# Square products in the fox gates of a two-layer hybrid trunk

## The chip, the cores and the metric

One core of a Trainium2 chip runs the whole program. The metric is device time in microseconds (us) of one execution. PE is the matmul engine (TensorE), DVE is VectorE, ACT is ScalarE, POOL is GpSimd, SP is the engine whose queue issues the weight loads.

## The reference, cut to what matters

The model has two layers, 256 rows, a width of 2048, all float32. The change touches how one half of the mixer's gate, `sigmoid(g_fox)`, is computed:

```
a = rms_norm(x, n_mix_pre)
proj = a @ w_in                      # the last 4096 columns of it are g_fox, g_nsa (2048 each)
o_fox, o_nsa = fox_attention(...), nsa_attention(...)      # 256 x 1024 each
mix = sigmoid(g_fox) * (o_fox @ w_up_fox) + sigmoid(g_nsa) * (o_nsa @ w_up_nsa)
x = x + rms_norm(mix @ w_out, n_mix_post)
a = rms_norm(x, n_ffn_pre)
h = (silu(a @ w_gate) * (a @ w_up)) @ w_down
return x + rms_norm(h, n_ffn_post)
```

## The kernel before, in words

**Split products.** Every float32 operand is split into a high and a low part (a fast matmul type each), and each product becomes three matmuls, high times high, high times low, low times high (lines 394 to 396 in `part`, 441 to 443 in `product`). The rows of an activation are in two tiles of 128, `t` = 0 and 1. `aT[t][c]` holds the mixer's input transposed: four tiles of 128 k rows, high and low. The 2048 inner rows are 16 k tiles.

**Weight units.** `stream` (line 242) cuts a weight into units of two k tiles by 512 columns (512 KB). SP loads a unit into one of five raw buffers; ACT copies it to the high part `wh`, DVE subtracts it for the low part `wl` (lines 162 and 172, which are those of the helpers `copy` and `split`). How far ahead of PE this is written into the program is set by `budget`: `room["ahead"]` units ahead at most, `room["slots"]` live buffers at most. `ensure(i)` is called once for each unit and row tile that PE uses, and emits a step or two of the next units' splits.

**A chunk** (`chunk`, line 408) is one block of 512 columns: both row tiles in two PSUM banks, 96 matmuls for 16 k tiles. After each part (6 matmuls) `pump` takes one step of a side generator.

**A square** (`square_chunk`, line 445) works on two column blocks at once. Two k tiles, two row tiles and two column blocks are a 2 by 2 by 2 product; instead of 8 products it takes 7 (of 3 matmuls each) with sums of rows and sums of weights as operands. A "pair" is the two units of both column blocks with the same two k tiles. The first `SEVEN` = 2 pairs are squares, unless `lead` puts some plain pairs ahead of them. Then `between` gathers the 7 banks into the four results (`gather`, line 665), and the other pairs follow plainly, 24 matmuls each, into four banks. The sums of weights are made by `split_sums` (line 259) in two steps: step 1 makes the parts of the left unit (`wl`) and of one tile of the right one (`wq`) and four sums in the raw buffers (lines 268 and 276 to 279 in the profile); step 2 makes the parts of the two sums, `xh`, `xl`, `yh`, `yl`, all under the names `wh` and `wl`. The products come in the order 6, 5, 7, ..., and product 6 takes `yh` and `yl`. The sums of rows are made by `left_gen` (line 1177).

**Alike rows.** A square mixes two row tiles, whose rows have different norm factors. In the feed-forward stage `powers`, `spread` and `alike` (lines 1398 to 1422) therefore multiply `aT2` by the power of two in each row's factor, in place, before squares are used.

**The mixer's gates and ups.** The loop at line 1207 goes through `n` (nsa) and `f` (fox). For each of four column blocks `c` of 512 it runs the gate chunk (16 k tiles, 96 matmuls; ACT takes the sigmoid out of PSUM, line 1216) and the up chunk (8 k tiles of `oT`, 48 matmuls; DVE multiplies it by the gate, line 1221 for n, 1223 and 1224 for f, where the product is added into `mix`). After each f block `mix_gen` transposes `mix` for the output projection (PSUM tile `mT`, SBUF tile `mixT`); for c = 3 it rests two pumps first (`REST`). The output projection `out` begins with two plain pairs (`lead` = 2). Its row sums come from `left_gen(1, mixT, ...)`: the tiles `full` and `sm`.

**The end of a layer.** `tail` closes the last down projection with `turn(0)` and `turn(1)`, generators which make the next layer's `aT`, one per row tile; PE waits for those tiles at the start of layer two.

Engines run their own instructions in the order in which the program was written; the order is set by hand (`tc.manual_schedule`), by `pump`, `ensure` and `need`.

Of the kernel before, what the change touches and what calls it, by code (L numbers as in the profile page):

```python
# [38 lines left out]
KT = DM // 128  # L39
# [9 lines left out]
ROOM_OUT = 10  # L49
ROOM_LATE = 22  # L50
REST = 2
ROOM_MIX = 16
ROOM_DOWN = 10

# [54 lines left out]
def trunk(ctx: ExitStack, tc: tile.TileContext, I: dict, consts: bass.AP, out: bass.AP):  # L109
# [879 lines left out]
        yield  # L989


    def squares(left, right, k0, nk, own=False, skew=0, lead=0):


        ks = range(k0, k0 + nk, 2)
        pairs = [[None, None] for k in ks]
        level = len(ks) - skew
        order = [(p, i) for p in range(level) for i in range(2)]
        order += [(p, i) for i in range(2) for p in range(level, len(ks))]
        for p, i in order:  # L1000
            w, col = (left, right)[i]
            pairs[p][i] = stream(w, ks[p], 2, col, 512)[0]
        for g, u in pairs[lead:lead + SEVEN]:
            units[g].update(block=u, own=own)
            units[u]["second"] = True
        return pairs

    def plan(l):
# [38 lines left out]
    def run_layer(l, P, aT, rs, turns, x_src, x_mid, x_next):  # L1047
# [126 lines left out]

        sums = {}

        def left_gen(c, rows, home):

            n = 2 * SEVEN
# [21 lines left out]
                pass  # L1201

        def lhs_s(f, p):
            i = (5, 6, 7, 3).index(f)
            return sums["hi"][:, i, p, :], sums["lo"][:, i, p, :]

        for nm in ("n", "f"):
            if nm == "f":
                budget(8)
            for c in range(4):  # L1210
                ga, ua = P[nm][c]
                sgc = [None, None]

                def gate_evac(t, p):
                    sgc[t] = staged([128, 512], F32, "sgc")
                    act.activation(sgc[t], p, AF.Sigmoid, scale=rs[t][:, 0:1])

                def up_evac(t, p):
                    m = mix[t][c // 2][:, (c % 2) * 512:(c % 2) * 512 + 512]
                    if nm == "n":  # L1220
                        dve.tensor_tensor(m, p, sgc[t], op=OP.mult)
                    else:
                        dve.tensor_tensor(sgc[t], p, sgc[t], op=OP.mult)
                        dve.tensor_tensor(m, m, sgc[t], op=OP.add)

                chunk(ga, lhs_a, gate_evac)
                if nm == "f" and c == 3:
                    room["slots"], room["ahead"] = ROOM_MIX, 5
                if c == 0:
                    drain()  # L1230
                    if nm == "n":
                        for h in range(FH):
                            waiting.append(fox_head(L, h))
                chunk(ua, lhs_o(L["onsa"] if nm == "n" else L["ofox"]), up_evac)
                if nm == "f":
                    made = [Once(mix_gen(t, c, REST * (c == 3))) for t in range(2)]
                    waiting.extend(made)
                    if c == 2:
                        lefts = Once(left_gen(1, mixT, slot))
                        waiting.append(lefts)  # L1240

        close_stage()
        open_stage(f"ffn{l}")

        def one(shape, dt, name):
            return staged(shape, dt, name, 1)

        def tagged(tag, bufs=2):

            return lambda shape, dt, name: staged(shape, dt, tag, bufs)  # L1250


        due = deque()
# [31 lines left out]
        def tail(couples, lhs, yg, partial, wait, gen, loads, xs, gb, last=False, lead=0):  # L1285
# [64 lines left out]
        lefts.need("end")  # L1350

        def load_late():
            load_rows(x_src, tagged("wq"))()
# [35 lines left out]
            waiting.extend(late)  # L1389
            late.clear()  # L1390

        rest = [None, None]

        p2 = [None, None]

        def powers(t):
            p2[t], rest[t] = staged([128, 1], F32, "p2"), staged([128, 1], F32, "rest")
            r = rs2[t][:, 0:1].bitcast(I32)  # L1400
            dve.tensor_scalar(p2[t].bitcast(I32), r, 0x7F800000, None, op0=OP.bitwise_and)
            dve.tensor_scalar(rest[t].bitcast(I32), r, 0x007FFFFF, 0x3F800000, op0=OP.bitwise_and, op1=OP.bitwise_or)

        def spread():
            for _ in range(6):
                yield
            tp = side_ps("rb")
            for t in range(2):
                pe.transpose(tp[:, t * 128:(t + 1) * 128], p2[t].to_broadcast([128, 128]), ident)
            sums["rb"] = staged([128, 2, 128], F32, "rb", 1)  # L1410
            dve.tensor_copy(sums["rb"], tp[:, 0:256].rearrange("p (t n) -> p t n", t=2))
            yield "rb"

        def alike(have, j):

            if j < 4 or j % 2:
                return
            have.need("rb")
            rb = sums["rb"]
            for c, t in [(c, t) for c in range(j // 2 - 1 if j > 4 else 0, j // 2) for t in range(2)]:  # L1420
                a = aT2[t][c].rearrange("p k s n -> p (k s) n")
                dve.tensor_tensor(a, f32(a), rb[:, t:t + 1, :].to_broadcast([128, 8, 128]), op=OP.mult)

        (a0, a1), (b0, b1) = FFN_PARTS

        def ffn(c):
# [4 lines left out]
            if c < 2:  # L1431
                ga, ua = P["ffn"][c]
                scale = rest if c else rs2

                def gate_evac(t, p):
                    if c == 0:
                        turns2[t].need("rs")
                        powers(t)
                    act.activation(hb[:, t], p, AF.Silu, scale=scale[t][:, 0:1])

                def up_evac(t, p):
                    dve.scalar_tensor_tensor(hb[:, t], p, scale[t][:, 0:1], hb[:, t], op0=OP.mult, op1=OP.mult)

                if c:
                    chunk(ga, lhs_a2, gate_evac)
                    left_sums(0, aT2, one)
                    chunk(ua, lhs_a2, up_evac)
                else:
                    chunk(ga, lhs_a2, gate_evac, before=wait_a2, head=8)
                    drain()  # L1450
                    budget(8, 8)
                    have = Once(spread())
                    waiting.append(have)
                    chunk(ua, lhs_a2, up_evac, after=lambda j: alike(have, j))
                    alike(have, 8)
# [151 lines left out]
```

## Time and profile before

| | us |
|---|---|
| median of 3 runs | 2807.79 (2807.76 to 2807.98) |
| profiled execution, device time | 2807.83 |
| its span in the trace | 2806.0 |
| PE busy | 2792.1 |
| DVE busy | 1995.7 |
| ACT busy | 1426.3 |
| POOL busy | 106.3 |

The profiled execution is 0.04 us above the median; 1.8 us of it lie outside the traced span. Busy times are averages over stages that differ. PE's matmuls overlap in the trace: each is shown with 390 ns, but in a steady stream they start closer together, so a group's busy time divided by its count is less than the length of one row.

### The profile page before, as it was taken

To read this page: it belongs to the slowest core of one execution; us is meant where nothing else is said; L and a number is where in the kernel's file an instruction comes from. 1 tells how busy PE (TensorE), PEld (TensorE's weight loads), DVE (VectorE), ACT (ScalarE), POOL (GpSimd) and SP (SyncE) were. 2 spreads that over 40 slices of the span, in tenths; PEclk is the share of its full clock that TensorE was granted. 3 is DMA by queue.
4 is the path that set the end of the run, shared out by engine and by line. 5 is a ranking of instruction groups with operands and counts; after the bars stand their busy time and mean duration, and the time that the engine had idled before them with its cause. 6 is when DMAs were issued, how large, how long until landed. Compare 5 with 4: busy or idle time off the path is not lost.

```text
span 2806.0 us, 35561 instructions
## 1 busy us (share of the span) xinstructions
PE 2792.1 (100%) x13114; PEld 2338.9 (83%) x13114; DVE 1995.7 (71%) x2578; ACT 1426.3 (51%) x2022; POOL 106.3 (4%) x191
## 2 busy tenths in 40 slices
PE   9999999999999999999999999999999999999998
PEld 8988888888888888888899888888888888888887
DVE  6666665576888788788666566555768887887885
ACT  6555554455554455445455455544564544544453
POOL 0100000001000000000011000000020000000000
PEclk9999999999999999999999999999999999999999
DMA  7673446566565566556666644455765655665564
GB/s 249 201 261 116 140 151 199 196 222 224 195 224 170 167 220 217 175 191 220 215 201 224 218 130 147 154 198 188 239 219 190 214 178 183 217 202 173 188 218 165
DMA packets 291806, 547.04 MB, mean 195 GB/s; under 512 B 17264, under 2 KB 59568, under 8 KB 291632
## 3 DMA queue, kind: packets, MB, share of 16 engines
q1 hardware_dynamic: 289856, 543.56, 58.9%
q8 instruction: 103, 1.69, 0.2%
q10 hardware_dynamic: 1776, 1.21, 0.1%
q14 instruction: 71, 0.58, 0.1%
HBM read 536.31 MB, written 8.39 MB: 194 GB/s over the span
## 4 chain that ended last, share of the span: by engine, by line
PE 98%; DVE 1%; DMA 0%; ACT 0%; issue 0%; POOL 0%; SPq 0%; DVEq 0%; ACTq 0%; POOLq 0%
PE acc L443 16%; PE acc L441 16%; PE acc L442 16%; PE acc L394 15%; PE acc L396 15%; PE acc L395 15%; PE hT L526 1%; PE ph L881 1%; PE ph L880 1%; PE tp L526 0%; PE ns L706 0%; PE ns L705 0%; PE no L699 0%; PE no L698 0%; PE no L700 0%; DMA raw<-in_w_in 0%
## 5 line engine op out<-in xcount | busy, mean ns | idle before, releaser
L162 ACT ACTIVATE wh<-raw 128x1024 fp32r<-128x1024 f32 (+1 forms) x1064 | 1067.6, 1044 | 470.1 <-DVE raw L277 158.1
L172 DVE TENSOR_TENSOR wl<-raw,wh 128x1024 fp32r<-128x1024 f32 (+1 forms) x896 | 1049.3, 1208 | 295.4 <-ACT wh L162 266.6
L394 PE MATMUL acc<-wh,aT 128*128 128x512 f32 (+1 forms) x1534 | 598.0, 390 | 0.0
L396 PE MATMUL acc<-wh,aT 128*128 128x512 f32 (+1 forms) x1534 | 585.1, 381 | 1.0 <-DVE aT L575 1.0
L395 PE MATMUL acc<-wl,aT 128*128 128x512 f32 (+1 forms) x1534 | 584.9, 381 | 0.1
L441 PE MATMUL acc<-wh,aT 128*128 128x512 f32 x972 | 381.5, 392 | 0.0
L443 PE MATMUL acc<-wh,aT 128*128 128x512 f32 x972 | 379.0, 390 | 0.0
L442 PE MATMUL acc<-wl,aT 128*128 128x512 f32 x972 | 378.4, 389 | 0.0
L396 PEld LDWEIGHTS acc<-wh,aT 128*128 128x128 f32 x1534 | 287.9, 188 | 51.5 <-DVE aT L575 1.7
L394 PEld LDWEIGHTS acc<-wh,aT 128*128 128x128 f32 x1534 | 288.4, 188 | 43.9 <-issue 0.8
L395 PEld LDWEIGHTS acc<-wl,aT 128*128 128x128 f32 x1534 | 288.6, 188 | 41.8 <-DVE wl L172 0.3
L441 PE MATMUL acc<-wh,hT 128*128 128x512 f32 x624 | 243.9, 391 | 0.0
L443 PE MATMUL acc<-wh,hT 128*128 128x512 f32 x624 | 243.3, 390 | 0.0
L442 PE MATMUL acc<-wl,hT 128*128 128x512 f32 x624 | 243.0, 389 | 0.0
L268 DVE TENSOR_TENSOR wl<-raw,wh 128x1024 fp32r<-128x1024 f32 x168 | 202.4, 1221 | 22.6 <-PE acc L442 9.9
L443 PEld LDWEIGHTS acc<-wh,aT 128*128 128x128 f32 x972 | 182.4, 188 | 38.6
L442 PEld LDWEIGHTS acc<-wl,aT 128*128 128x128 f32 x972 | 182.6, 188 | 37.4
L441 PEld LDWEIGHTS acc<-wh,aT 128*128 128x128 f32 x972 | 182.5, 188 | 37.0
L442 PEld LDWEIGHTS acc<-wl,hT 128*128 128x128 f32 x624 | 117.2, 188 | 24.7
L443 PEld LDWEIGHTS acc<-wh,hT 128*128 128x128 f32 x624 | 117.1, 188 | 24.6
L441 PEld LDWEIGHTS acc<-wh,hT 128*128 128x128 f32 x624 | 117.2, 188 | 24.4
L394 PE MATMUL acc<-wh,oT 128*128 128x512 f32 x256 | 102.0, 399 | 0.0
(351 smaller groups left out, 3082.7 us busy)
## 6 DMA issues: line engine op xcount, KB each, us to landing
raw<-in_w_in SPq DMA_DIRECT2D x224, 512.0 KB, 4.6
raw<-in_w_ffn_gate SPq DMA_DIRECT2D x176, 512.0 KB, 4.8
raw<-in_w_ffn_up SPq DMA_DIRECT2D x176, 512.0 KB, 4.7
raw<-in_w_ffn_down SPq DMA_DIRECT2D x176, 512.0 KB, 5.7
raw<-in_w_in SPq DMA_DIRECT2D x96, 432.0 KB, 4.4
raw<-in_w_out SPq DMA_DIRECT2D x64, 512.0 KB, 5.7
raw<-in_w_up_nsa SPq DMA_DIRECT2D x32, 512.0 KB, 4.6
raw<-in_w_up_fox SPq DMA_DIRECT2D x32, 512.0 KB, 4.9
```

The source lines that it names most:

```text
L162: act.activation(o, i, AF.Copy, scale=1.0 if scale is None else scale)
L172: dve.tensor_tensor(lo, src, f32(hi), op=OP.subtract)
L268: dve.tensor_tensor(lo, src, f32(hi), op=OP.subtract)
L394: pe.matmul(ps[t][:, :n], ah, hi, start=first, stop=False)
L395: pe.matmul(ps[t][:, :n], ah, lo, start=False, stop=False)
L396: pe.matmul(ps[t][:, :n], al, hi, start=False, stop=end)
L441: pe.matmul(ps, ah, bh, start=first, stop=False)
L442: pe.matmul(ps, ah, bl, start=False, stop=False)
L443: pe.matmul(ps, al, bh, start=False, stop=last)
L526: pe.transpose(dst[:, j * 128:(j + 1) * 128], s, ident)
L880: pe.matmul(ph[:120, 0:256], b, units[u]["hi"][:, jj, :], start=p == 0, stop=False)
L881: pe.matmul(ph[:120, 0:256], b, units[u]["lo"][:, jj, :], start=False, stop=p == CL - 1)
```

## The change

For the fox gates the four gate chunks become two couples of column blocks, (0, 1) and (2, 3). Each couple is one `square_chunk` with two squares and no lead, then come its two up chunks. The weight sums are marked `own` (their `wq` lives in the common slots). For this `powers`, `spread` and `alike` become methods that take the tiles; they are used on `aT` beside the nsa gates of c = 2, and `left_gen(0, aT, ...)` makes the row sums beside the nsa gates of c = 3. `alike` is 8 multiplications of 128 x 1024 (4, 2, 2 at three places) in each layer; `spread` adds two transposes on PE and one copy on DVE. The split of weights runs up to 6 units ahead in place of 4 in the fox stage. `turn(1)` at a layer's end now first finishes `turn(0)` up to its fourth tile. The wait for the sums of `mixT` moves into `lhs_s`.

```diff
@@ plan
             for c in range(4):
-                a = stream(w, 0, KT, col + 512 * c, 512)
+                a = None
+                if nm == "n":
+                    a = stream(w, 0, KT, col + 512 * c, 512)
+                elif c % 2 == 0:
+                    a = squares((w, col + 512 * c), (w, col + 512 * c + 512), 0, KT, True)
                 P[nm].append((a, stream(I[up][l], 0, 8, 512 * c, 512)))
@@ run_layer
-                chunk(ga, lhs_a, gate_evac)
...
+        scaled = [powers(rs[t]) for t in range(2)]
+        rows_by = [rs[t][:, 0:1] for t in range(2)]
+        for c in range(4):
+            ga, ua = P["n"][c]
...
+            if c == 2:
+                chunk(ga, lhs_a, gate_evac, after=lambda j: alike(aT, have, rb, j))
+                alike(aT, have, rb, 8)
+                rows_by = [v[:, 0:1] for _, v in scaled]
+            else:
+                chunk(ga, lhs_a, gate_evac, beside=left_gen(0, aT, tagged("kT")) if c == 3 else None)
...
+            chunk(ua, lhs_o(L["onsa"]), up_evac)
+        budget(ROOM_F // 2, 6)
+        for c in range(4):
+            ga, ua = P["f"][c]
+            if not c % 2:
...
+                def between(ps):
+                    gather(ps, sg_, tagged("w2", 1)([128, 1, 512], F32, "hu"), False)
+
+                def gate_evac(t, right, p):
+                    o = sg_[t][right]
+                    dve.tensor_tensor(o, p, o, op=OP.add)
+                    act.activation(o, o, AF.Sigmoid, scale=rows_by[t])
+
+                square_chunk(ga, lhs_a, lhs_s, between, gate_evac, together=False)
...
+            if c == 3:
+                room["slots"], room["ahead"] = ROOM_MIX, 5
+            chunk(ua, lhs_o(L["ofox"]), up_evac)
+            made = [Once(mix_gen(t, c, REST * (c == 3))) for t in range(2)]
...
@@ tail, turn
+                if t:
+                    turns[0].need("3")
                 turns[t] = Once(gen(t, ys, ssy[t], xs))
```

Three places show how the rows move. The first is DVE at the start of the fox stage; `mix_2988` and `mix_2990` are the last nsa up block's results for row tiles 0 and 1. Before:

```order
L172 TENSOR_TENSOR wl<-raw,wh 128x1024 x12
L1221 TENSOR_TENSOR mix_2988<-acc_4270,sgc 128x512
L1221 TENSOR_TENSOR mix_2990<-acc_4271,sgc 128x512
L172 TENSOR_TENSOR wl<-raw,wh 128x1024 x13
L1223 TENSOR_TENSOR sgc<-acc_4502,sgc 128x512
```

and after, where lines 269 and 277 to 280 are `split_sums`:

```order
L173 TENSOR_TENSOR wl<-raw,wh 128x1024 x4
L269 TENSOR_TENSOR wl<-raw,wh 128x1024
L269 TENSOR_TENSOR wq<-raw,wq 128x512
L277 TENSOR_TENSOR raw<-raw 128x512
...
L1263 TENSOR_TENSOR mix_2988<-acc_4303,sgc 128x512
L1263 TENSOR_TENSOR mix_2990<-acc_4304,sgc 128x512
L269 TENSOR_TENSOR wl<-raw,wh 128x1024 x3
L269 TENSOR_TENSOR wq<-raw,wq 128x512
L277 TENSOR_TENSOR raw<-raw 128x512
L278 TENSOR_TENSOR raw<-raw 128x512
L279 TENSOR_TENSOR raw<-raw 128x512
L280 TENSOR_TENSOR raw<-raw 128x512
L269 TENSOR_TENSOR wl<-raw,wh 128x1024 x2
```

Step 1 of the first square stands ahead of the two `mix` rows; its step 2 (the first two of the three `wl`), the whole step 1 of the second square and its step 2 (the last two `wl`) stand behind them. The second place is PE at the same point of the program, after the change; `kT` is the tag in which the sums of `aT` lie:

```order
L397 MATMUL acc_4304<-wh,oT 128x512
L442 MATMUL acc_4385<-wh,kT 128x512
L443 MATMUL acc_4385<-wl,kT 128x512
L444 MATMUL acc_4385<-wh,kT 128x512
```

The last up matmul of row tile 1 (`acc_4304`) is followed at once by product 6 of the first square; before, the plain gate chunk stood there. The third place is DVE beside the last fox up chunk, ahead of the output projection; `mix_2988` and `mix_2990` are now the last fox block's. Before:

```order
L172 TENSOR_TENSOR wl<-raw,wh 128x1024 x7
L268 TENSOR_TENSOR wl<-raw,wh 128x1024
L268 TENSOR_TENSOR wq<-raw,wq 128x512
...
L1223 TENSOR_TENSOR sgc<-acc_5246,sgc 128x512
L1224 TENSOR_TENSOR mix_2988<-mix_2988,sgc 128x512
L1223 TENSOR_TENSOR sgc<-acc_5247,sgc 128x512
```

and after, where `qT` is the tag of the right block's gates:

```order
L173 TENSOR_TENSOR mixT<-mT,mixT 128x4x128 x2
L173 TENSOR_TENSOR wl<-raw,wh 128x1024 x2
L1223 TENSOR_TENSOR full<-mixT 128x512 x2
L269 TENSOR_TENSOR wl<-raw,wh 128x1024
L269 TENSOR_TENSOR wq<-raw,wq 128x512
...
L1228 TENSOR_TENSOR sm<-full 128x256
L1229 TENSOR_TENSOR sm<-sm,full 128x256
L1303 TENSOR_TENSOR qT<-acc_5321,qT 128x512
L1304 TENSOR_TENSOR mix_2988<-mix_2988,qT 128x512
L1231 TENSOR_TENSOR sm<-full 128x256
L1232 TENSOR_TENSOR sm<-full,sm 128x256
L1303 TENSOR_TENSOR qT<-acc_5322,qT 128x512
```

The transposed block of c = 2 and the row sums for the output projection (`full`, `sm`) used to stand beside the gate chunk of c = 3; they now stand beside the up chunk, ahead of and between the rows that read the up chunk's two banks.

## Rows read from the trace of the kernel before

**Rows 1.** The page: busy times, and the chain that ended last.
```profile
PE 2792.1 (100%) x13114; PEld 2338.9 (83%) x13114; DVE 1995.7 (71%) x2578; ACT 1426.3 (51%) x2022; POOL 106.3 (4%) x191
...
PE 98%; DVE 1%; DMA 0%; ACT 0%; issue 0%; POOL 0%; SPq 0%; DVEq 0%; ACTq 0%; POOLq 0%
```

**Rows 2.** PE's waits: total us, times, longest us.
```profile
PE acc L396 <- DVE aT L575: 1.0, 2, 0.8
```

**Rows 3.** Three stretches: busy time of each engine, clock, DMA share, GB/s.
```profile
398.00:432.00 34.00, 34.00 (x179) 28.70 (x179) 21.21 (x35) 20.08 (x34) 0.00 (x0) 1.00 0.55 170
600.00:620.00 20.00, 20.00 (x94) 16.57 (x93) 19.02 (x22) 11.05 (x14) 0.00 (x0) 1.00 0.63 205
1408.00:1418.00 10.00, 8.92 (x49) 7.57 (x48) 8.27 (x18) 8.37 (x24) 8.32 (x15) 1.00 0.41 111
```

**Rows 4.** Timeline of PE, last fox up chunk into output projection: start, length.
```profile
586.41 0.39 PE L394 MATMUL acc<-wh,oT 128*128 128x512 f32 x1
...
597.29 0.39 PE L441 MATMUL acc<-wh,mixT 128*128 128x512 f32 x1
...
600.01 0.39 PE L441 MATMUL acc<-wh,mixT 128*128 128x512 f32 x1
```

**Rows 5.** Timeline of PE around the two transposes of `spread`, feed-forward stage.
```profile
718.74 0.39 PE L396 MATMUL acc<-wh,aT 128*128 128x512 f32 x1
...
719.42 0.40 PE L395 MATMUL acc<-wl,aT 128*128 128x512 f32 x1
```

**Rows 6.** Timeline of PE at the start of layer two.
```profile
1411.46 0.46 PE L396 MATMUL acc<-wh,aT 128*128 128x432 f32 x1 [0.24 <-DVE aT L575]
...
1416.06 0.46 PE L396 MATMUL acc<-wh,aT 128*128 128x432 f32 x1 [0.79 <-DVE aT L575]
```

**Rows 7.** Timeline of DVE at the same place.
```profile
1409.73 1.41 DVE L609 SCALAR_TENSOR_TENSOR smh<-yg,ry,smh 128x512 f32<-128x512 f32 x2 [2.21 <-POOL ry L541]
```

**Rows 8.** Timeline of PE, first matmuls of the fox gates, layer one.
```profile
463.88 0.39 PE L394 MATMUL acc<-wh,aT 128*128 128x512 f32 x1
464.10 0.39 PE L395 MATMUL acc<-wl,aT 128*128 128x512 f32 x1
```

**Rows 9.** Timeline of DVE at the same place.
```profile
464.07 0.69 DVE L1221 TENSOR_TENSOR mix<-acc,sgc 128x512 f32<-128x512 f32 x1 [0.67 <-PE acc L396]
464.68 2.35 DVE L172 TENSOR_TENSOR wl<-raw,wh 128x1024 fp32r<-128x1024 f32 x2
```

**Rows 10.** Timeline of DVE, end of the fox ups into the output projection.
```profile
597.64 0.68 DVE L1223 TENSOR_TENSOR sgc<-acc,sgc 128x512 f32<-128x512 f32 x1
598.35 0.69 DVE L1224 TENSOR_TENSOR mix<-mix,sgc 128x512 f32<-128x512 f32 x1
598.96 0.68 DVE L1223 TENSOR_TENSOR sgc<-acc,sgc 128x512 f32<-128x512 f32 x1
...
600.29 3.48 DVE L268 TENSOR_TENSOR wl<-raw,wh 128x1024 fp32r<-128x1024 f32 x3
...
607.20 2.50 DVE L268 TENSOR_TENSOR wl<-raw,wh 128x1024 fp32r<-128x1024 f32 x2
```

**Rows 11.** Timeline of ACT over the same stretch.
```profile
586.62 0.69 ACT L1216 ACTIVATE sgc<-acc,rs 128x512 f32<-128x512 f32 x1 [0.67 <-PE acc L396]
...
593.46 0.63 ACT L162 ACTIVATE wq<-raw 128x512 fp32r<-128x512 f32 x1 [1.41 <-DMA raw<-in_w_out]
...
607.38 2.01 ACT L162 ACTIVATE wh<-raw 128x1024 fp32r<-128x1024 f32 x2 [0.39 <-DVE raw L279]
```

**Rows 12.** Timeline of PE, transposes of a `mix` block after a first gate part.
```profile
497.88 0.60 PE L526 MATMUL mT<-ct,mix 128*128 128x128 f32 x4
```

**Rows 13.** Timeline of DVE after the second row tile's `mixT`.
```profile
501.93 4.63 DVE L172 TENSOR_TENSOR wl<-raw,wh 128x1024 fp32r<-128x1024 f32 x4 [0.26 <-ACT wh L162]
```

**Rows 14.** Instructions on the tile `full`: ns min/median/max, first and last start.
```profile
L1188 DVE TENSOR_TENSOR sm<-full x10: 418/425/427, 573.7 to 2635.9; 128x256 f32<-128x256 f32 x10
...
L1183 DVE TENSOR_TENSOR full<-mixT x4: 684/686/686, 571.4 to 1966.4; 128x512 f32<-128x512 f32 x4
```

**Rows 15.** Timeline of DVE, `alike` in the feed-forward stage.
```profile
720.86 4.62 DVE L1422 TENSOR_TENSOR aT<-aT,rb 128x1024 fp32r<-128x1024 f32 x4
```

More of the change, by code (lines that the diff above doesn't have):

```diff
@@ L989, in gates_gen, with powers, spread, alike @@
         yield
+    def powers(factor):
+        p2, left = small([128, 1], F32, "p2"), small([128, 1], F32, "rest")
+        r = factor[:, 0:1].bitcast(I32)
+        dve.tensor_scalar(p2.bitcast(I32), r, 0x7F800000, None, op0=OP.bitwise_and)
+        dve.tensor_scalar(left.bitcast(I32), r, 0x007FFFFF, 0x3F800000, op0=OP.bitwise_and, op1=OP.bitwise_or)
+        return p2, left
+    def spread(p2, rb):
+        for _ in range(6):
+            yield
+        tp = side_ps("rb")
+        for t in range(2):
+            pe.transpose(tp[:, t * 128:(t + 1) * 128], p2[t].to_broadcast([128, 128]), ident)
+        dve.tensor_copy(rb, tp[:, 0:256].rearrange("p (t n) -> p t n", t=2))
+        yield "rb"
+    def alike(a, have, rb, j):
+        if j < 4 or j % 2:
+            return
+        have.need("rb")
+        for c, t in [(c, t) for c in range(j // 2 - 1 if j > 4 else 0, j // 2) for t in range(2)]:
+            v = a[t][c].rearrange("p k s n -> p (k s) n")
+            dve.tensor_tensor(v, f32(v), rb[:, t:t + 1, :].to_broadcast([128, 8, 128]), op=OP.mult)
     def squares(left, right, k0, nk, own=False, skew=0, lead=0):
@@ L1175, in run_layer, with one, tagged @@
         sums = {}
+        def one(shape, dt, name):
+            return staged(shape, dt, name, 1)
+        def tagged(tag, bufs=2):
+            return lambda shape, dt, name: staged(shape, dt, tag, bufs)
         def left_gen(c, rows, home):
@@ L1203, in lhs_s @@
         def lhs_s(f, p):
+            if "gen" in sums:
+                sums.pop("gen").need("end")
             i = (5, 6, 7, 3).index(f)
             return sums["hi"][:, i, p, :], sums["lo"][:, i, p, :]
[L1207 to L1224, printed above, removed]
-                chunk(ga, lhs_a, gate_evac)
-                if nm == "f" and c == 3:
-                    room["slots"], room["ahead"] = ROOM_MIX, 5
-                if c == 0:
-                    drain()
[L1231 to L1240, printed above, removed]
@@ L1242, in run_layer @@
         close_stage()
         open_stage(f"ffn{l}")
[L1245 to L1250, printed above, removed]
         due = deque()
@@ L1349, in run_layer @@
         g2 = (2 + l) * 16
-        lefts.need("end")
         def load_late():
@@ L1390, in hand_on @@
             late.clear()
[L1394 to L1422, printed above, removed]
+        p2, rest = [None, None], [None, None]
         (a0, a1), (b0, b1) = FFN_PARTS
@@ L1437, in gate_evac @@
                         turns2[t].need("rs")
-                        powers(t)
+                        p2[t], rest[t] = powers(rs2[t])
                     act.activation(hb[:, t], p, AF.Silu, scale=scale[t][:, 0:1])
@@ L1451, in ffn @@
                     budget(8, 8)
-                    have = Once(spread())
+                    rb = one([128, 2, 128], F32, "rb")
+                    have = Once(spread(p2, rb))
                     waiting.append(have)
-                    chunk(ua, lhs_a2, up_evac, after=lambda j: alike(have, j))
-                    alike(have, 8)
+                    chunk(ua, lhs_a2, up_evac, after=lambda j: alike(aT2, have, rb, j))
+                    alike(aT2, have, rb, 8)
                 made_of(c, hb, 0 if c else 3)
```

28 lines of the change are left out of this document (added).

## The prediction

> **What bounds the kernel now.** I read the page first: PE is busy for the whole span and makes up 98% of the chain that ended last [rows 1]. A busy PE need not be a PE at its peak, so I looked next at what PE waits for. The longest entry beside the start-up is 1.0 us in two pieces, for `aT` [rows 2], and the timeline puts both at the start of layer two [rows 6]. So the time is the number of matmuls times their spacing, and a saved matmul counts in full, as long as no new wait appears. The spacing is not the 390 ns of a row: between the first matmul of the last fox up chunk and the first one of the output projection lie 48 matmuls and 597.29 - 586.41 = 10.88 us [rows 4], 0.227 us each. The products of the output projection have the same spacing: twelve matmuls from 597.29 to 600.01 take 2.72 us [rows 4].
>
> The second question is how much slack the engines have that feed PE. Over the span DVE is at 71%, but where squares are prepared it is close to full: 19.02 of 20 us from 600 to 620 [rows 3]. That stretch serves two squares at the start of the output projection, which has two plain pairs ahead of them as cover. The change builds the same thing twice more in each layer, and with no lead.
>
> **The change, part by part.** The sum is made against 2807.83 us, the profiled execution, which stands 0.04 us above the median.
>
> *Matmuls saved.* A square takes 7 products in place of 8, so 3 matmuls less. Two squares in each of two couples in each of two layers are 24 matmuls: 24 x 0.227 = -5.45 us. Both ends are close, since the spacing is the same on either side of 597.29, in `part` and in `product`.
>
> The Trainium skill, "TensorE: Matmul & The Clock Gate", section "Back-to-back issue gap", gives a sustained spacing of about 131 ns for a matmul of 512 columns; by it the saving would be an estimated 24 x 0.131 = 3.1 us. The trace disagrees with 227 ns, and the trace decides.
>
> *Transposes added.* `spread` puts two transposes on PE. In the feed-forward stage two matmuls that they part start 719.42 - 718.74 = 0.68 us apart in place of 0.454 [rows 5]; that is 0.23 a layer, **+0.45 us**.
>
> *Alike rows.* Eight multiplications a layer, four of which take 4.62 us [rows 15], about 9.2 us, beside the nsa gates and ups of c = 2. There DVE is busy for 21.21 of 34 us [rows 3], so it has room for them on the whole; but four come in one piece, ahead of fox-head steps for which PE waits in order. DVE's idle time there is 12.8 us, in pieces. I take 0.15 us a layer; the bounds are 0 and 3, the latter if two thirds of one 4.62 piece lands on PE. **+0.3 us.** The row sums (`left_gen`) have a whole gate chunk before they are wanted and are costed at nothing; their cover is that chunk's 96 x 0.227 = 21.8 us against some 5 us of work.
>
> *The couple's first square, first wait.* Product 6 of the first square follows the last nsa up matmul at once. Its first matmul takes `yh`; its second takes `yl`, which DVE makes as the second row behind the up chunk's last `mix` row. That `mix` row cannot start before PE ends the bank: it starts at 464.07 and the next DVE row starts at 464.68 [rows 9]. Two low parts take 2.35 us [rows 9], so `yl` is there at 467.04, where PE would want it at 464.10 [rows 8]. That is a wait of **2.9 us a layer**; between 2.3 (the products in a slightly better place) and 3.5 there is little room, since an engine's rows run in order. Nothing can hide it: PE's next matmul is the one that waits.
>
> The Trainium skill, "PSUM — Partial Sum Buffer", section "Engine vs sequencer instructions", says that the queues of ScalarE and VectorE are strictly first in, first out. That speaks against this change: `yl`, whose inputs are ready long before, cannot pass the `mix` row that waits for PE. The trace agrees as far as it goes: the `wl` row of 464.68 starts only behind the `mix` row that was released at 464.07. If the queue let `yl` pass, this wait would be 0.
>
> *The couple's second square.* Its step 1 and step 2 stand behind those two rows. The same sequence (three `wl`, `wq`, four sums, two `wl`) is in the trace at the output projection, from 600.29 to 607.20 + 2.50 = 609.70 [rows 10], 9.41 us. From 464.68 it ends at 474.1. PE gets there 21 matmuls behind the first square's second matmul, at 467.0 + 4.8 = 471.8. A wait of **2.3 us a layer**. ACT's copies for it end at 609.39 [rows 11], 9.1 us behind the same start, so they would not save it. Bounds 0 (if DVE gains what ACT's waits cost it here) and 3.5.
>
> The second couple starts from an up chunk that ended a whole couple later, but its squares were split earlier (6 units ahead); the sums are there before PE wants them by my count, to a few tenths. Nothing for it; the bounds are 0 and 2.
>
> *The mixT of c = 0.* The two ups of a couple now follow each other, so the transposes of c = 0 come after the first part of the up chunk of c = 1, 10.88 + 1.36 = 12.24 us after the first up chunk starts. The `mix` row they need stands on DVE behind step 1 of the second couple's first pair. In the trace the same queue (sigmoid, five copies, `wl`, `wq`, four sums, then `mix`) runs from 586.62 to 598.35 + 0.69 = 599.04 [rows 10, 11], 12.42 us, of which ACT waits 1.41 us for a weight. After the change DVE first adds the plain part to the gate, so the sigmoid starts some 0.9 us into the chunk: 13.3 us. A wait of **1.1 us a layer**, bounds 0 (no wait for the weight) and 2.5.
>
> *The output projection's lead.* It takes a bank of the last up chunk for its third accumulator: PE wants it 600.01 - 586.41 = 13.60 us after that chunk starts, and DVE frees it with the multiplication of 598.96 + 0.68 = 599.64 [rows 4, 10]. That is only 0.37 us of slack. After the change the transposes of c = 2 come into this chunk (about 0.9 us on PE), so it is wanted at 14.5. DVE has more ahead of it: the second `mixT` of a block is done 501.93 - (497.88 - 1.36) = 5.4 us after the chunk in which it is made starts [rows 12, 13] (1.36 is the first part, six matmuls). Then come two `wl` (2.3), two `full` (1.3), step 1 (607.20 - 600.29 - 2.3 = 4.6), two `sm` (0.8), a multiplication and an addition of row tile 0 (1.3), two `sm` (0.8) and the multiplication itself (0.7) [rows 9, 10, 14]: 17.2 us. A wait of **2.7 us a layer**, bounds 0.7 and 4.
>
> *The layer boundary.* `turn(0)` is finished before `turn(1)` starts, which puts two additions of 1.41 us together [rows 7] behind the `aT` parts for which PE waits [rows 6]. The two waits show 0.24 and 0.79 us of idle time, with the broken pipeline about 1.66 us. I take **-1.0 us**, once, bounds -1.66 and 0.
>
> *The sum.* 2 x (0.15 + 2.9 + 2.3 + 1.1 + 2.7) = +18.3; saved -5.45; transposes +0.45; boundary -1.0. In all **+12.3**, so 2820.1 us. All lower bounds together give 2 x (0 + 2.3 + 0 + 0 + 0.7) - 5.45 + 0.45 - 1.66 = -0.7, or 2807.2; all upper ones 2 x (3 + 3.5 + 3.5 + 2 + 2.5 + 4) - 5 = +32, or 2839.8.
>
> **Rivals.**
>
> *The waits aren't there.* DVE's rows run earlier than I count, and PE finds all sums ready: -5.45 + 0.45 - 1.0 = -6.0, 2801.8 us, faster. For it speaks that PE now waits for almost nothing and that DVE has 29% of the span idle. Against it stands that the first wait follows from order alone. It turns faster by more than 0.2% only if all waits together stay under 0.4 us.
>
> *Only one pair of the waits comes.* Only those of the first square: 2 x 5.2 - 6.0 = +4.4, 2812.2 us. Only those at the ups and the lead: 2 x 3.8 - 6.0 = +1.6, 2809.4. Either is within 0.2%. For it: the second pair rests on an ACT wait and on pump order, the second square on DVE's pace.
>
> *The alike rows cost more,* 3 in place of 0.15 us a layer with the rest as counted: +18.0, 2825.8 us. The fox heads are a chain through ACT, DVE and PE, and each link is short; against it, DVE's share there.
>
> *The clock falls in the waits.* PE's rest of up to 3 us may lower its clock for a while. At the layer boundary, where PE is busy for 8.92 of 10 us and rests up to 0.79 us, the granted clock shows 1.00 [rows 3], the 2.4 GHz level. Nothing in the trace shows a rest of 3 us in the middle. If one microsecond at the lower level, 1.2 GHz, costs half a microsecond, a few us in each of four places add 2 to 8 us: 2822 to 2828.
>
> **How the numbers follow.** A difference of 0.2%, 5.6 us, is about what a measurement of this kernel can tell from no change. All waits as counted, 0.65: slower, 2820.1. Costlier alike rows or a lower clock, 0.12: slower. Only one pair of the waits, 0.18: 0.15 within 0.2% and 0.03 above. No waits, 0.05: faster. That makes faster 0.05, same 0.15, slower 0.80. The range from 2811 to 2827 leaves out the case without waits, half of the one with a pair of them, and the far end of the lower clock; it takes in single bounds of the sum (-5 when the second square doesn't wait, +6 by alike).
>
> **What the profile would show.** If I am right, PE's waits name `wl` of `split_sums` (line 269) twice at the start of the fox stage in each layer, near 3 and 2 us, the multiplication that frees a bank (line 1303) once, near 2.7 us, and `mix` (line 1304) near 1 us; the count of PE rows in the fox gates falls by 24; the `aT` waits at the start of layer two shrink. I am wrong if these waits are under half a us, if `wl` is ready because the two ACT copies and DVE's low parts run before the last up chunk ends, or if PE waits somewhere else, in the fox heads above all.

## The result

The changed kernel takes 2825.34 us (median of 6 runs, 2825.11 to 2827.91) against 2807.89 us before (6 runs, 2807.73 to 2808.16): 17.45 us more, a ratio of 1.0064 (95% interval 1.0053 to 1.0074). Slower was forecast, at 2820.1 within 2811 to 2827. One execution, of the kernel a_even below, was disturbed throughout and took 8422.82 us; its median leaves it out.

The page of the changed kernel, busy times and chain, answers to [rows 1].

```profile
PE 2786.8 (99%) x13094; PEld 2332.3 (83%) x13094; DVE 2080.6 (74%) x2698; ACT 1449.9 (51%) x2048; POOL 105.3 (4%) x191
...
PE 92%; DVE 4%; DMA 1%; ACT 1%; issue 1%; POOL 0%; SPq 0%; DVEq 0%; ACTq 0%; POOLq 0%
```

PE has 20 instructions fewer (24 matmuls less, 4 transposes more) and is busy for 5.3 us less, yet the span is longer: PE's share of the chain falls from 98% to 92%. PE's waits (total us, times, longest) answer to [rows 2], where one entry of 1.0 us stood for the whole body of the program.

```profile
PE acc L443 <- DVE wl L269: 7.3, 5, 2.8
PE acc L442 <- DVE qT L1303: 4.9, 2, 2.4
PE mT L527 <- DVE yg L669: 2.9, 2, 1.6
PE fpt L527 <- DVE P L742: 2.6, 4, 1.1
PE mT L527 <- DVE mix L1304: 1.9, 2, 1.0
PE acc L442 <- ACT wh L163: 1.9, 2, 0.9
...
PE acc L442 <- DVE mixT L173: 1.0, 2, 0.5
...
PE acc L397 <- DVE aT L576: 0.6, 1, 0.6
```

The entries repeat from layer to layer, but for the first, whose fifth wait, 0.16 us idle, stands in the feed-forward stage. The first, second and fifth were forecast, and with the first, as part of the second square's wait, what the sixth stands for. The third, fourth and seventh were not; the fourth is a wait in the fox heads, which the prediction had named as a sign of being wrong. The view counts only the time in which PE is idle; below, a wait is the distance between two starts less the usual 0.227 us.

The first square on PE, layer one, answers to [rows 8]:

```profile
466.74 0.39 PE L442 MATMUL acc<-wh,kT 128*128 128x512 f32 x1
469.95 0.51 PE L443 MATMUL acc<-wl,kT 128*128 128x512 f32 x1 [2.82 <-DVE wl L269]
...
474.42 0.39 PE L444 MATMUL acc<-wh,aT 128*128 128x512 f32 x1
475.74 0.50 PE L442 MATMUL acc<-wh,kT 128*128 128x512 f32 x1 [0.93 <-ACT wh L163]
477.00 0.50 PE L443 MATMUL acc<-wl,kT 128*128 128x512 f32 x1 [0.76 <-DVE wl L269]
477.33 0.39 PE L444 MATMUL acc<-wh,kT 128*128 128x512 f32 x1
```

and the same place on DVE, to [rows 9]:

```profile
466.94 0.69 DVE L1263 TENSOR_TENSOR mix<-acc,sgc 128x512 f32<-128x512 f32 x1 [0.67 <-PE acc L397]
467.54 3.49 DVE L269 TENSOR_TENSOR wl<-raw,wh 128x1024 fp32r<-128x1024 f32 x3
...
474.45 2.49 DVE L269 TENSOR_TENSOR wl<-raw,wh 128x1024 fp32r<-128x1024 f32 x2
```

Product 6 waits for `yl` for 469.95 - 466.74 - 0.23 = 2.98 us; the second square waits 1.09 for `yh` and 1.03 for `yl`, 2.12 together. DVE does exactly the chain that was read from the trace of before, three rows, a whole step 1 and two rows, behind a `mix` row that PE itself released.

At the output projection PE shows two more:

```profile
606.62 0.39 PE L444 MATMUL acc<-wh,mixT 128*128 128x512 f32 x1
609.45 0.47 PE L442 MATMUL acc<-wh,mixT 128*128 128x512 f32 x1 [2.44 <-DVE qT L1303]
...
629.66 0.39 PE L444 MATMUL acc<-wh,mixT 128*128 128x512 f32 x1
631.43 0.66 PE L527 MATMUL mT<-ct,mix 128*128 128x128 f32 x4 [1.38 <-DVE yg L669]
```

The first is the bank of the third accumulator, 2.60 us. The second is a transpose of the last `mix` block for row tile 1, which now comes behind both squares and takes a bank that `gather` (line 669) has yet to read: 1.54 us.

### The profile page after: what moved, and what is told of

Its sections match the earlier page's. It is cut to its first block, busy times and chain, and to the rows that moved or that the text cites. A ratio compares the mean times of both kernels' runs of the same rounds, so it can differ in the third digit from the quotient of the medians.

```text
span 2823.7 us, 35595 instructions
## 1 busy us (share of the span) xinstructions
PE 2786.8 (99%) x13094; PEld 2332.3 (83%) x13094; DVE 2080.6 (74%) x2698; ACT 1449.9 (51%) x2048; POOL 105.3 (4%) x191
## 4 chain that ended last, share of the span: by engine, by line
PE 92%; DVE 4%; DMA 1%; ACT 1%; issue 1%; POOL 0%; SPq 0%; DVEq 0%; ACTq 0%; POOLq 0%
PE acc L443 17%; PE acc L444 17%; PE acc L442 16%; PE acc L395 12%; PE acc L397 12%; PE acc L396 12%; DVE wl L173 1%; DMA raw<-in_w_in 1%; PE hT L527 1%; ACT wh L163 1%; PE ph L882 1%; PE ph L881 1%; DVE wl L269 1%; DMA raw<-in_w_out 0%; PE tp L527 0%
## 5 line engine op out<-in xcount | busy, mean ns | idle before, releaser
L163 ACT ACTIVATE wh<-raw 128x1024 fp32r<-128x1024 f32 (+1 forms) x1072 | 1080.1, 1044 | 499.9 <-DVE raw L278 185.7
L173 DVE TENSOR_TENSOR wl<-raw,wh 128x1024 fp32r<-128x1024 f32 (+1 forms) x880 | 1033.9, 1209 | 226.1 <-ACT wh L163 191.6
L395 PE MATMUL acc<-wh,aT 128*128 128x512 f32 (+1 forms) x1278 | 498.1, 390 | 0.0
L397 PE MATMUL acc<-wh,aT 128*128 128x512 f32 (+1 forms) x1278 | 485.5, 380 | 0.7 <-DVE aT L576 0.6
L396 PE MATMUL acc<-wl,aT 128*128 128x512 f32 (+1 forms) x1278 | 485.4, 380 | 0.0
L442 PE MATMUL acc<-wh,aT 128*128 128x512 f32 x1188 | 465.3, 392 | 0.0
L444 PE MATMUL acc<-wh,aT 128*128 128x512 f32 x1188 | 462.8, 390 | 0.0
L443 PE MATMUL acc<-wl,aT 128*128 128x512 f32 x1188 | 462.6, 389 | 0.0
L397 PEld LDWEIGHTS acc<-wh,aT 128*128 128x128 f32 x1278 | 239.8, 188 | 41.2 <-DVE aT L576 1.4
L395 PEld LDWEIGHTS acc<-wh,aT 128*128 128x128 f32 x1278 | 240.4, 188 | 34.0 <-issue 0.8
L396 PEld LDWEIGHTS acc<-wl,aT 128*128 128x128 f32 x1278 | 240.5, 188 | 31.9 <-DVE wl L173 0.2
L444 PEld LDWEIGHTS acc<-wh,aT 128*128 128x128 f32 x1188 | 223.0, 188 | 46.6
L443 PEld LDWEIGHTS acc<-wl,aT 128*128 128x128 f32 x1188 | 223.1, 188 | 45.5
L442 PEld LDWEIGHTS acc<-wh,aT 128*128 128x128 f32 x1188 | 223.1, 188 | 45.4
L269 DVE TENSOR_TENSOR wl<-raw,wh 128x1024 fp32r<-128x1024 f32 x192 | 231.5, 1221 | 22.3 <-ACT wh L163 9.8
```

The lines of the kernel that those rows point to most:

```text
L163: act.activation(o, i, AF.Copy, scale=1.0 if scale is None else scale)
L173: dve.tensor_tensor(lo, src, f32(hi), op=OP.subtract)
L269: dve.tensor_tensor(lo, src, f32(hi), op=OP.subtract)
L395: pe.matmul(ps[t][:, :n], ah, hi, start=first, stop=False)
L396: pe.matmul(ps[t][:, :n], ah, lo, start=False, stop=False)
L397: pe.matmul(ps[t][:, :n], al, hi, start=False, stop=end)
```

## The experiments

All are timed in 5 rounds against the kernel before, which took 2807.86 to 2807.98 us beside them. Names with b_ start from the kernel before, with a_ from the changed one. Two theories are tried. **Order and cover**: each wait is the place of a row in DVE's or ACT's queue, and goes when that place or the cover ahead of it changes. **Pace**, the rival: DVE is short of time in the whole fox stage, and a wait removed comes back later. A third question came from the comparison of the traces: in the feed-forward stage, which the change does not touch, the changed kernel is faster.

**Where tiles lie.** One square of the feed-forward stage, the first of its 42 matmuls and the plain one behind the last, in the kernel before

```profile
862.48 0.40 PE L441 MATMUL acc<-wh,smh 128*128 128x512 f32 x1
...
872.16 0.39 PE L441 MATMUL acc<-wh,aT 128*128 128x512 f32 x1
```

and in the changed one:

```profile
874.13 0.39 PE L442 MATMUL acc<-wh,smh 128*128 128x512 f32 x1
...
883.65 0.39 PE L442 MATMUL acc<-wh,aT 128*128 128x512 f32 x1
```

9.68 us against 9.52: 230.4 ns a matmul against 226.7, with no wait in either. There are 26 such stretches in the two layers; in the kernel before 14 run at 230.4 ns and 12 at 232.8, after the change 25 run at 226.7 and one has a short wait in it. In sum the faster spacing is 5.2 us. The only thing there that the change altered is where four tiles of 128 x 1 (`p2`, `rest`) come from, which moves the common slots by 128 bytes and the sums of rows `smh`, `sml` not at all.

```diff
-            p2[t], rest[t] = staged([128, 1], F32, "p2"), staged([128, 1], F32, "rest")
+            p2[t], rest[t] = small([128, 1], F32, "p2"), small([128, 1], F32, "rest")
```

> The kernel before, with nothing but its four 128 x 1 tiles p2 and rest taken from the small pool in place of the stage's pool, as the change does in passing. This moves all common slots (and the raw buffers) up by 128 bytes and leaves the row sums smh and sml of the feed-forward stage where they were. Theory one (place): the matmuls of the feed-forward squares run at 226.7 ns in place of 230.4 to 232.8, because stationary sums and moving weights then lie a multiple of 512 bytes apart; 26 square stretches of 42 matmuls by 3.7 to 6.1 ns give -5.2 us, so 2802.6 us. Theory two (schedule): the faster squares after the change come from the order of work, and this kernel takes 2807.8.

Measured: 2802.85 us, 0.9982 (0.9973 to 0.9991). The same, with tiles of 128 x 16 each:

> As b_pad128, but with tiles that move the slots up by 256 bytes. Theory one (place, a multiple of 512 bytes apart is what counts): slots and sums are again not a multiple of 512 apart (128 the other way), so the squares stay at 230 to 233 ns and the time at 2807.8, within 1.5. If any shift of the slots helps, 2802.6. Theory two (schedule): 2807.8 as well; the two are told apart by b_pad128.

Measured: 2806.74 us, 0.9996 (0.9987 to 1.0004). And the changed kernel with the line the other way round:

> The changed kernel with p2 and rest in the stage's pool, so that slots lie where they lay before the change. Theory one (place): the feed-forward squares fall back to 230 to 233 ns and the time rises by 5.2 to 2830.5 us; the squares of the fox gates may change as well, by 8 stretches of 42 matmuls by a few ns, 1 us at most. Theory two (schedule): 2825.3, no change.

Measured: 2829.97 us, 1.0078 (1.0065 to 1.0091), 4.6 above the changed kernel. The same stretch in b_pad128

```profile
862.63 0.39 PE L441 MATMUL acc<-wh,smh 128*128 128x512 f32 x1
...
872.15 0.39 PE L441 MATMUL acc<-wh,aT 128*128 128x512 f32 x1
```

and in b_pad256:

```profile
862.30 0.40 PE L441 MATMUL acc<-wh,smh 128*128 128x512 f32 x1
...
871.95 0.39 PE L441 MATMUL acc<-wh,aT 128*128 128x512 f32 x1
```

9.52 and 9.65 us. The schedule is that of the kernel before in both; only the place differs. Theory two (schedule) falls. That it is the distance between the two operands, and not the place of the slots by itself, shows at the output projection: there the sums of rows lie in common slots too and move with the weights, and the squares take 9.52 us, 226.7 ns a matmul, in the kernel before, in b_pad128 and in b_pad256 alike.

**The layer boundary.** The changed kernel without `turns[0].need("3")`:

```diff
-                if t:
-                    turns[0].need("3")
```

> The changed kernel without the line that finishes turn(0) before turn(1) starts. Theory: the waits at the start of layer two come back as they were before the change (1.66 us lost in place of 0.75), so +0.9 us, 2826.2. Rival: the line changes nothing that lasts, since PE regains it in the next wait: 2825.3.

Measured: 2826.20 us, 1.0065 (1.0053 to 1.0078). The intervals don't part it from the changed kernel; its trace shows PE's two waits for `aT` at the start of layer two again, 0.21 and 0.79 us idle, as in [rows 6], where the changed kernel has one of 0.58. The size fits the 1.0 us of the prediction and isn't shown more closely.

**Cover for the first squares.**

```diff
-                    a = squares((w, col + 512 * c), (w, col + 512 * c + 512), 0, KT, True)
+                    a = squares((w, col + 512 * c), (w, col + 512 * c + 512), 0, KT, True, 0, 2)
...
-left_gen(0, aT, tagged("kT"))
+left_gen(1, aT, tagged("kT"))
...
-square_chunk(ga, lhs_a, lhs_s, between, gate_evac, together=False)
+square_chunk(ga, lhs_a, lhs_s, between, gate_evac, together=False, lead=2)
```

> The changed kernel with two plain pairs ahead of the squares in both couples (lead 2, row sums of aT's second quarter). Theory (the order of DVE's queue, no cover for the first squares): 48 plain matmuls, 10.9 us, stand ahead of product 6, so the two waits of 3.0 and 2.1 us on wl of split_sums in each layer go: -10.2 us. The transposes of c = 1 now come beside the lead and may wait some 1 us a layer. 2815 to 2818 us. Rival (DVE's pace): DVE is short of time in the whole stage, the waits only move to the second square or the gather, and the time stays within 3 us of 2825.3.

Measured: 2813.44 us, 1.0019 (1.0011 to 1.0028): 11.9 us less than the changed kernel, and 1.6 less than the forecast's range. Its longest waits on PE are

```profile
PE acc L442 <- DVE qT L1303: 4.9, 2, 2.4
PE mT L527 <- DVE yg L669: 2.6, 2, 1.8
PE fpt L527 <- DVE P L742: 2.6, 4, 1.1
```

The waits for `wl` of `split_sums` are gone from the view, those for the transposes of c = 0, which the theory had left standing, too, and the others stand much as they were. DVE does the same work in the same stage; the rival falls for this place.

**The fox heads.** Two edits, alone and together. First `spread` without its turn in the side queue:

```diff
-                waiting.append(have)
+                have.need("rb")
```

> The changed kernel with the two transposes of spread written at once at the end of the first nsa gate chunk, in place of a side generator that stands ahead of the fox heads and takes seven of their pumps. Theory: the fox heads end as early as before, no sigmoid comes between the last head's exponentials, the table load of 1.28 us leaves the chain, and the waits of fpt on P (0.36 and 1.25 us a layer) go: -3.2 us, 2822.1. Rival: the waits come from the eight alike multiplications on DVE beside the heads and stay: 2825.3.

Measured: 2824.52 us, 1.0060 (1.0048 to 1.0073). A miss: the heads' waits didn't go, they changed their name.

```profile
PE fs L706 <- DVE qkT L173: 2.1, 2, 1.0
...
PE fo L700 <- DVE PT L173: 0.6, 2, 0.3
```

DVE's rows ahead of `qkT` there begin with the block of four `alike` multiplications; one `wl` row stands between the two:

```profile
407.25 4.62 DVE L1018 TENSOR_TENSOR aT<-aT,vc 128x1024 fp32r<-128x1024 f32 x4
```

In the changed kernel the last head's exponentials fall behind the sigmoid of c = 2 instead, so that ACT has to change its function table in the middle of the head's chain:

```profile
436.80 1.28 ACT L695 ACT_TABLE_LOAD   x1 [2.09 <-DVE fnm L737]
438.10 0.37 ACT L695 ACTIVATE P<-fs,fnm 128x128 f32<-128x128 f32 x1
```

The second edit breaks the block up; a_even has it alone, a_alike has both.

```diff
-                chunk(ga, lhs_a, gate_evac, after=lambda j: alike(aT, have, rb, j))
-                alike(aT, have, rb, 8)
+                def one_alike(n):
+                    v = aT[n % 2][n // 2].rearrange("p k s n -> p (k s) n")
+                    dve.tensor_tensor(v, f32(v), rb[:, n % 2:n % 2 + 1, :].to_broadcast([128, 8, 128]), op=OP.mult)
+                chunk(ga, lhs_a, gate_evac, after=lambda j: one_alike(j - 2) if j > 1 else None)
+                one_alike(6)
+                one_alike(7)
```

> The changed kernel with the alike multiplications one at a time, and spread still a generator ahead of the fox heads. If the table load in the last head's chain is enough for the wait (in a_spread it was gone, and the rows of DVE made a wait of the same size), P's waits of 1.25 and 0.36 us a layer stay and the time is 2825, within 1. If the alike block is what makes the last head late as well, the waits fall as in a_alike, and the time is 2822.

Measured: 2824.78 us (the median of five, 2823.95 to 2826.53), 1.0060 (1.0046 to 1.0074). The time speaks for the first case. Its trace is of the execution of 8422.82 us, so no wait is read from it, but the order of its rows can be: it has 6 table loads ahead of exponentials of the fox heads (line 695), as the changed kernel has, where a_spread, a_alike and the kernel before have 4.

> The kernel a_spread, with the eight alike multiplications one at a time, one after each unit of the nsa gate chunk of c = 2 from the third on and the last two at its end, in place of four, two and two at once. Theory: the fox heads' waits (qkT 1.15 and PT 0.44 us a layer in a_spread, P 1.25 and 0.36 in the changed kernel) come from the 4.6 us block on DVE ahead of the heads' rows; with blocks of 1.2 us they fall to 0.4 us a layer or less: 2822.1 us. Rival: the heads are late for the table load or for other rows, and the waits stay: 2824.5.

Measured: 2821.84 us, 1.0049 (1.0036 to 1.0061): 3.5 below the changed kernel, 2.7 below a_spread. The waits of `P`, `qkT` and `fs` are gone from the view; 0.25 us a layer is left ahead of `fo`. So two causes stood one behind the other, the table load and the block on DVE: taking away one alone gives back 0.8 us (a_spread) or 0.6 (a_even), both together 3.5.

**The output projection.** Sums begun later:

```diff
-            made = [Once(mix_gen(t, c, REST * (c == 3))) for t in range(2)]
-            waiting.extend(made)
-            if c == 2:
-                sums["gen"] = Once(left_gen(1, mixT, slot))
-                waiting.append(sums["gen"])
+            made = [Once(mix_gen(t, c)) for t in range(2)]
+            if c == 3:
+                sums["gen"] = Once(left_gen(1, mixT, slot, True))
+                waiting.append(sums["gen"])
+            waiting.extend(made)
```

(`True` makes `left_gen` yield three times in place of five.)

> The changed kernel with the row sums for the output projection begun only after the last fox up chunk, ahead of the transposes of c = 3, in three steps in place of five, and no rest for those transposes. Theory: DVE frees the bank for the third accumulator in time (2.6 us a layer gone), both row tiles are transposed before the squares (1.5 gone) and bank 7 is read in time (0.66 gone): -9.6 us at best, 2815.7; half of it if the sums are now late for the first square by up to 2 us a layer, 2820. Rival: the waits at the output projection are DVE's pace, and the sum of them stays within 3 us.

Measured: 2830.27 us, 1.0080 (1.0066 to 1.0094), slower by 4.9. A miss. The three waits go, but one for the sums of rows takes their place:

```profile
PE acc L442 <- ACT smh L163: 9.8, 2, 4.9
```

By the distance of starts it is 5.04 us a layer, and the three were 4.80 and 4.98 together, so the waits themselves come out nearly even. Most of the 4.9 us comes behind them, where PE goes on at a lower granted clock. From the first square of layer one:

```profile
621.00:626.00 5.00, 4.86 (x11) 3.38 (x12) 4.95 (x6) 4.39 (x7) 0.00 (x0) 0.50 0.64 200
```

The clock (behind POOL) is 0.50, the 1.2 GHz level, right behind a rest of 4.87 us; from 621.10 on 13 matmuls take 6.08 us, 3.1 more than at 0.227 us each, and in layer two 8 matmuls take 2.1 more, some 0.3 of it a wait for the sums' low part (`sml`).

> All three together (lead 2, spread at once, row sums of the output projection late), and one pump of rest for the transposes of c = 0 and 1. Theory: the waits of the first squares, the fox heads, the output projection and the first mixT go, -10.2 - 3.2 - 9.6 - 2.2 = -25.2 us: 2800 us, faster than the kernel before by 7 to 8; with a few new small waits 2803. Rival: DVE's pace keeps half of it: 2813.

Measured: 2818.78 us, 1.0039 (1.0026 to 1.0051). A miss for both, 16 us above the theory and 6 above the rival. The same 4.9 us wait stands there twice, with 2.8 and 3.0 us of slow matmuls behind it as in a_out, and the fox heads wait as in a_spread (2.1 and 0.6 us in the view). Between the last fox up chunk and the first square DVE has step 1 and step 2 of two squares, the sums of rows and the last `mix` rows to do, and two plain pairs cover it in neither of the two orders tried. The next kernel therefore gives more cover, four plain pairs:

```diff
-        P["out"] = [squares((w, 0), (w, 512), 0, KT, True, 0, 2),
+        P["out"] = [squares((w, 0), (w, 512), 0, KT, True, 0, 4),
...
-                sums["gen"] = Once(left_gen(1, mixT, slot))
+                sums["gen"] = Once(left_gen(2, mixT, slot))
...
-            made = [Once(mix_gen(t, c, REST * (c == 3))) for t in range(2)]
+            made = [Once(mix_gen(t, c, (1, 1, 0, REST)[c])) for t in range(2)]
```

(and lead=4 in the call of `tail`, with the load of the gains moved to the fourth pair.)

> a_lead and a_alike together, one pump of rest for the transposes of c = 0 and 1, and four plain pairs ahead of the squares of the output projection in place of two, with the row sums of mixT's third quarter. Theory (order and cover): DVE's step 1 for those squares now comes behind the rows that free the last up chunk's banks, both row tiles of c = 3 are transposed in the longer lead, and the sums have 22 us in place of 11: the waits at the output projection (5 us a layer in a_lead) and at the fox heads (1.6) go, 2813.4 - 10 - 3.2 = 2800.2 us; with small new waits 2803. That is below the kernel before (2807.9) by the 24 matmuls less, 5.4, and the faster feed-forward squares, 5.0, less some 3 of small things. Rival (DVE's pace in the stage): half of the waits stay, 2807.

Measured: 2800.09 us, 0.9972 (0.9962 to 0.9983), as the theory had it. Several things were changed at once, so the kernel shows that the waits can be covered together, and not which edit covered which. What is left of PE's waits behind the start:

```profile
PE acc L443 <- DVE wl L269: 0.7, 1, 0.7
...
PE acc L397 <- DVE aT L576: 0.6, 1, 0.6
PE acc L442 <- DVE qT L1308: 0.4, 2, 0.2
```

Last, the place of the row sums of the fox gates:

```diff
-        L["kT"] = [staged([128, 2, 528], F32R, "kT") for g in range(NG)]
+        L["kT"] = [staged([128, 2, 576], F32R, "kT") for g in range(NG)]
```

> a_best4 with the two kT tiles 4608 bytes long in place of 4224, so that the row sums of the fox gates, which take their place, lie a multiple of 512 bytes from the slots that hold the weights. Theory (place): the fox gates' squares run at 226.7 ns in place of 229.2, 8 stretches of 21 to 22 x 2 matmuls by 2.5 ns, -0.4 to -0.9 us against a_best4. Rival: the 229.2 ns are the start-up after a wait, and nothing changes.

Measured: 2799.45 us, 0.9971 (0.9960 to 0.9981). The second couple's squares, first matmul and the plain one behind them, take 552.17 - 542.54 = 9.63 us in a_best4

```profile
542.54 0.39 PE L442 MATMUL acc<-wh,kT 128*128 128x512 f32 x1
...
552.17 0.39 PE L442 MATMUL acc<-wh,aT 128*128 128x512 f32 x1
```

and 9.52 in a_best4k:

```profile
542.57 0.39 PE L442 MATMUL acc<-wh,kT 128*128 128x512 f32 x1
...
552.09 0.39 PE L442 MATMUL acc<-wh,aT 128*128 128x512 f32 x1
```

The spacing falls from 229.2 to 226.7 ns, as expected. That is 0.11 us in each of four couples, 0.4 us in all (the expectation counts eight stretches); the difference of the medians, 0.64 us, is inside the spread of the runs.

## Why the prediction was right, and where its sum was not

The direction, the cause and the range held: 24 matmuls were saved, and waits on DVE's queue cost more than they gave. That the time lies inside the range is in part luck. a_unpad, the same change without the gain in the feed-forward stage, which no step of the prediction names, takes 2829.97 us, above the range's end of 2827.

- **First square, 2.9 us a layer**: 2.98 measured. **Second square, 2.3**: 2.12, in two halves, the first of them for ACT's `yh`. **mixT of c = 0, 1.1**: 1.09 in layer one and 1.18 in layer two (`mix`, line 1304). **The lead's bank, 2.7**: 2.60. All four were read from [rows 8 to 14] as chains of rows in one queue, and each came out within 0.2 us. a_lead shows the cause of the first two: with cover ahead they are gone. The third is gone there too, and the fourth in a_out, where the sums no longer stand ahead of its row.
- **The matmuls saved and added**: the counts are as forecast, by the instructions on the page.
- **The boundary, -1.0**: the trace shows some 0.9; the timing can't confirm it.
- **Alike rows, 0.15 us a layer: the step that failed.** The block was priced by DVE's idle share [rows 3], which says how much work fits in, not who waits meanwhile. The fox heads lost 0.36 + 1.25 = 1.6 us a layer, about half of what the rival with 3 us gave them. That the rows added to the side queue push the last head behind a sigmoid, with a table load in its chain, was not seen at all. The bounds, 0 to 3, did hold it.
- **Missing terms.** The transposes of row tile 1 of the last block, pushed behind the squares by the row sums that stand in the side queue (1.54 and 1.71 us), and product 7's wait for the bank of row tile 0's transposes (0.66 and 0.67). The prediction followed DVE's queue there, and not the order in which `pump` hands out turns.
- **The feed-forward stage, nothing: -5.2 us.** No step mentions that moving `powers` moves all the slots. a_unpad and b_pad128 show this gain by itself.
- **The rival of the clock** forecast 2822 to 2828 and would have fitted the time, but the profiled execution, at 2825.52 us, has a mean granted clock of 0.999, as the kernel before has, and shows 1.00 from 470.00 to 474.00, right behind the rest of 3 us. So the clock isn't in this sum. In a_out it is.

Put together: 25.5 us of waits, -5.45 + 0.45 for the matmuls, -0.9 at the boundary and -5.2 in the feed-forward stage give +14.4; measured are 17.45. Of the 3.0 us between, the fox gates' squares at 229.2 ns explain 0.4 (4 stretches of 42 matmuls, 2.5 ns each), and the wider spacing after each of sixteen restarts (0.33 us from 477.00 on, in place of 0.227; behind transposes 0.06 to 0.12 us more than without a wait) explains some 1.6 by its first step alone; about 1.0 stays open. So the forecast of +12.3 was 5 us low: the waits came out 7.2 us above the forecast 18.3, the spacing and the open rest added 3.0, and the gain of 5.2 in the feed-forward stage took as much off again.

The waits that can be covered say what the change is worth: a_best4k is 8.4 us below the kernel before, of which b_pad128 has 5.1 without any of the change. About 3.3 us are left for everything else: the squares in the fox gates, the layer boundary's 0.9, the longer lead of the output projection and the small waits that remain. No run parts these.

## What to carry to other kernels

- A wait in a queue can be forecast to 0.2 us, as four were here, from the kernel before, if the same sequence of rows stands somewhere in its trace: count from the row that can't start earlier, and follow the side generators' turns as well as the engines' queues.
- A share of idle time prices neither a block in a queue nor its delay; ask which row stands directly behind the block and who waits for that one. Where a wait is removed and the time stays, look for a second cause of the same size before giving up the first.
- Work that has to be prepared on another engine needs plain work ahead of it. Here 11 us of plain matmuls covered the first squares, and 22 us those at the output projection, where 11 us had not been enough in either order. A rest that is moved can also grow dearer by the clock behind it (a_out).

## What the runs showed of the hardware that was not expected

**Matmul spacing depends on where the operands lie.** With the same instructions in the same order, squares run at 226.7 ns a matmul or at 229 to 233, by the distance between the stationary sums and the moving weights (stationary 128 x 128, moving 128 x 512; addresses from the sizes of the pools). The runs had it at a multiple of 512 bytes (226.7), 128 bytes off one way (230.4 and 232.8) and the other (229.8 and 232.1), and, in the fox gates, 256 bytes off for one part and 128 for the other (229.2). Whether 512 is the least distance that matters was not tried.

The Trainium skill, "SBUF — State Buffer", section "Operand start alignment", asks only that an operand start at a multiple of its element size, and says that its runs timed nothing; all the places here fulfil that, and the times differ by up to 2.7%.

**The clock fell after rests of 3 and 5 us; the first cost nothing, the second did.** In a_spread PE rests as above ahead of the first square's second matmul. Two stretches, its rest and what follows (busy times by engine, the clock behind POOL):

```profile
466.50:469.40 2.90, 0.16 (x1) 0.00 (x0) 2.90 (x4) 0.00 (x0) 0.00 (x0) 1.00 0.05 7
469.50:472.90 3.40, 3.40 (x8) 2.67 (x9) 3.30 (x5) 0.16 (x1) 0.00 (x0) 0.52 0.86 262
```

The granted clock is 0.52 for 3.4 us, near the 1.2 GHz level, and the 8 matmuls start 0.427 us apart. In the profiled execution of the changed kernel the same rest left it at 1.00. From the first square's first matmul to the second one's second it is 477.00 - 466.74 = 10.26 us in the changed kernel and 10.22 in a_spread: PE would have waited for `wl` at the end in any case. Behind the rest of 4.87 us in a_out and a_all no such wait follows, and the 2.1 to 3.1 us of slow matmuls are in the time.

**The table load** takes 1.28 us on ACT, in this chain between two rows of one softmax. The Trainium skill, "ScalarE: Activation LUTs", section "What ACT_TABLE_LOAD costs", gives about 1.28 us for it, and the trace agrees; the page adds a drain of 1.38 us for every switch, which the row behind (438.10, 1.30 us after the load's start) does not show here. In the kernel before, a load at 418.63 follows directly on a copy that ends at 418.62, and the next row starts at 419.93, so no such drain shows ahead of a load either.
